# Banded attention scores over all 128 rows with zero-padded keys, a 128-column rotary key projection, and five key slots

## The chip, the cores and the metric

The kernel runs on the 8 cores of one Trainium2 chip. Each core works on four of the 32 sequences and there is no communication. The metric is the device time of the slowest core, in microseconds (us).

Some executions fall into a second, slower state in which one die (cores 0 to 3 or 4 to 7) or both run at a lower granted TensorE clock. Two readings are therefore used. The first is the ratio of fast runs to fast runs. The second is what I call the *undisturbed-die mean*: the mean span of the four cores of a die, over the unprofiled executions in which that die's mean granted clock was 0.990 or more. It also uses the good die of a run whose other die was slow. It is not the metric: the slowest of eight cores lies some 10 to 20 us above it.

## The reference, cut to what matters

A decoder layer: half-step SwiGLU, two attention groups on one input projection (a latent-attention group "MLA" and a sliding-window group "SWA"), an output projection, another half-step SwiGLU. The two feed-forwards are most of the work. The part touched by the change is the scores of the sliding-window group:

```python
SWA_HEADS, SWA_KV_HEADS, SWA_HEAD_DIM, WINDOW = 8, 2, 64, 128

def swa_group(q, k, v, sinks, rel_bias):          # blocks of 128 queries
    q = q.reshape(B, nb, WINDOW, SWA_KV_HEADS, G, dh)      # dh = 64, G = 4
    kb, vb = band(k), band(v)                     # previous block + current block
    s = jnp.einsum('bnqhgd,bnkhd->bnhgqk', q, kb) * (dh ** -0.5)
    ...                                           # bias, mask, softmax with sinks, times vb

# mla_group: k_pe = rope(ckv_pe[..., KV_LORA:], cos, sin)  # 32 columns, shared by all heads
```

The scores contract over only 64 elements. The rotary key needs 32 projection columns, and another 32 for their rotated halves.

## The kernel before

The program is a list of operations put in order by a scheduler at build time; each engine then runs its own list in that order. The feed-forward of one tile (512 tokens) fills the gaps of the attention ("mixer") of another, so attention matmuls stand singly between long runs of feed-forward matmuls.

```python
VS, _ = sb("VS", [128, 8, 192], BF16)             # values, eight slots of 128 tokens
ksT, _ = sb("ksT", [128, 8, 128], BF16)           # keys: group 0 on rows 0-63, group 1 on rows 64-127
...
slot0 = (4 * ti) % 8                              # a tile fills four slots, the next tile the other four
...
proj(w, 192, 128, 64, bka)                        # rotary key projection, 64 columns of the array
k.tt("dve", t1[0:32, :], PS[bka][0:32, :], rope[0:32, 0, :], ALU.mult)
k.tt("dve", t2[0:32, :], PS[bka][32:64, :], rope[32:64, 1, :], ALU.mult)
...
k.copy("act", ksT[:, slot0:slot0 + 4, :].rearrange("p a b -> p (a b)"), PS[bk][:])
...
def swa_scores(q):                                # j: block of 128 queries, g: key-value group
    j, g = units[q]
    for wh in ([0] if 4 * ti + j > 0 else []) + [1]:      # previous block, own block
        kbs = (slot0 + j - 1 + wh) % 8
        _, sb_ = sbk.next()
        k.mm([(PS[sb_][:], ksT[64 * g:64 * g + 64, kbs, :],           # 64 rows of the array
               QS[64 * g:64 * g + 64, :, j * 128:(j + 1) * 128], True, True)])
        k.act(f_[:], PS[sb_][:], AF.Exp, scale=SC_SWA)
        ...
def wload(src, ncol, key):                        # a feed-forward weight tile
    i, w = wr.next()
    k.dma(f"w{i}", w[:, 0:ncol], src, [key], [w[:, 0:ncol]], ncol * 256, dv=-WLEAD)
```

The softmax here doesn't subtract the row's maximum and nothing guards it: scores larger than these inputs give would overflow.

Of the kernel before, what the change touches and what calls it, by code (L numbers as in the profile page):

```python
# [10 lines left out]
BF16 = mybir.dt.bfloat16  # L11
AF = mybir.ActivationFunctionType
ALU = mybir.AluOpType
# [14 lines left out]
WLEAD = 40.0  # L28
# [363 lines left out]
def build_program(NSEQ, debug=False):  # L392
# [26 lines left out]
    with contextlib.ExitStack() as es:  # L419
        es.enter_context(nc.allow_low_precision("bf16 matmul operands, fp32 accumulation"))  # L420
        sc = Sched(nc, es)
        k = K(sc)
        off = [16512]

        def sb(name, shape, dt, at=None):
            n = int(np.prod(shape[1:])) * (2 if dt == BF16 else 4)
            if at is None:
                o = (off[0] + 255) // 256 * 256
                off[0] = o + n
                assert off[0] <= 229344, (name, off[0])  # L430
            else:
                o = at
            t = sc.sb_at(name, shape, dt, o)
            return t, o

        KT, KT_o = sb("KT", [128, 8, S], BF16)
        VA, VA_o = sb("VA", [128, 16, 4, 192], BF16)
        VS, _ = sb("VS", [128, 8, 192], BF16)
        ksT, _ = sb("ksT", [128, 8, 128], BF16)
        EB, EB_o = sb("EB", [128, 2, 8, 128], F32)  # L440
        actb, _ = sb("act", [128, NFC, T], BF16)
        uF, _ = sb("uF", [128, 8, T], BF16)
        uM, uM_o = sb("uM", [128, 8, T], BF16)
        Nb, _ = sb("Nb", [128, 4, T], F32, at=uM_o)
        HB, HB_o = sb("HB", [128, 8, T], F32)
        QT, QT_o = sb("QT", [128, 8, T], BF16)
        uO, _ = sb("uO", [128, 8, T], BF16, at=QT_o)
        QS, QS_o = sb("QS", [128, 4, T], BF16)
        Db, D_o = sb("Db", [128, 4, T], F32)
        cqn, _ = sb("cqn", [128, 2, T], BF16, at=D_o)  # L450
        ckvn, _ = sb("ckvn", [128, T], BF16, at=D_o + 2048)
        kper, _ = sb("kper", [128, T], BF16, at=D_o + 3072)
        rope, _ = sb("rope", [128, 2, T], F32, at=D_o + 4096)
# [14 lines left out]
        sqb, _ = sb("sqb", [128, T], BF16)  # L468
        rsF, _ = sb("rsF", [128, T], F32)
        rsM, _ = sb("rsM", [128, T], F32)  # L470
        rsH, _ = sb("rsH", [128, T], F32)
        cst, _ = sb("cst", [128, 47], F32)
        esink, _ = sb("esink", [128, 4], F32)
        ones, _ = sb("ones", [128, 128], BF16)
        epsb, _ = sb("epsb", [128, 1], F32)
# [16 lines left out]
        PS = [sc.psum(i) for i in range(8)]  # L492
# [35 lines left out]
        a = first * ff  # L528
        for n in range(NT):
            b = min(st_[n + 1] * ff, starts[("F2", n)] - END)  # L530
            if n == 0:
                b = starts[("F2", 0)] - END
# [3 lines left out]
            a = max(b, 4 * ff)  # L536

        def vmap(f):
            v = f
            for a, b, m in windows:  # L540
                v += m * min(max((f - a) / (b - a), 0.0), 1.0)
            return v
# [17 lines left out]
        def load_x(ring, nm, src, key, dv=-8.0):  # L560
            i, t = ring.next()
            k.dma(f"{nm}{i}", t[:], src, [] if key is None else [key], [t[:]], 262144, dv=dv)
            return i, t
# [79 lines left out]

        def wload(src, ncol, key):
            i, w = wr.next()
            k.dma(f"w{i}", w[:, 0:ncol], src, [key], [w[:, 0:ncol]], ncol * 256, dv=-WLEAD)
            return w

        HBl = [HB[:, c, :] for c in range(8)]
# [36 lines left out]
        def ffn_thread():  # L686
# [3 lines left out]
            for ph, n, dur in phases:  # L690
# [36 lines left out]
                elif ph == "P":  # L727
                    for lc in range(NFC):
                        yield vmap(f0 + 2 * fgu * lc / NFC)
                        w = wload(wgu_s[0][lc], 2048, ("wgu", 0, lc))  # L730
                        gate_up(w, uFl, actl, lc, lc == 0)
                        gate_up(w, uF2, act2, lc)
# [3 lines left out]
                    for dc in range(8):  # L736
                        yield vmap(f0 + 2 * fgu + 2 * fdn * dc / 8)
                        ws = [wload(wd_s[0][2 * dc + hf], WD, ("wd", 0, 2 * dc + hf)) for hf in range(2)]
                        for q in range(2):
                            _, bk = fb.next()  # L740
                            for hf in range(2):
                                down_half(ws[hf], (actl, act2)[q], bk, hf)
                            f1_resid(n[q], dc, bk, sts[q])
# [33 lines left out]
        def bg_thread():  # L777
            yield vmap(2 * ff) + 0.5
            k.memset("pool", VA[:].rearrange("p b c e -> p (b c) e")[:, 0:16, 64:128], 1.0)
            k.memset("pool", VS[:, :, 64:128], 1.0)  # L780
            ebf = EB[:].rearrange("p w h q -> p (w h q)")
            k.dma("eb", ebf, relb_in, [], [ebf], 1 << 20)
            k.act(ebf, ebf, AF.Exp)
            k.mask(EB[:, 0], [[0, 8], [-1, 128]], -1, 1, ALU.is_ge)
            k.mask(EB[:, 1], [[0, 8], [1, 128]], 0, -1, ALU.is_ge)
            k.act(esink[:], cst[:, 43:47], AF.Exp)
# [21 lines left out]
        def wkeys(key):  # L808
            return [key, key + (0,), key + (1,)]

        def cload(p):
            i, w = cr.next()
            n = PIECES[p]
            k.dma(f"c{i}", w[:, 0:n], wm_s[p, :, 0:n], wkeys(("wm", p)), [w[:, 0:n]], n * 256, dv=-12.0)
            return w

        def mixer(n):
            si, ti = divmod(n, NTI)
            a, b, m = windows[n]
# [3 lines left out]
            def at(us=0.0):  # L823
                v = vmap(a + (b - a) * min(done[0] / tot, 1.0))
                done[0] += us
                return v
            c0 = ti * T
            slot0 = (4 * ti) % 8
            yield at(0)
            k.dma("rsM", rsM[:], rs_s[n], [("rs", n)], [rsM[:]], 262144, dv=-6.0)  # L830
            for c in range(8):
                _, t = load_x(xmr, "xm", h1_s[n, c], ("h1", n, c))
# [3 lines left out]
            def proj(w, ld, lo, M, bk):  # L836
                w3 = w[:, 0:8 * ld].rearrange("p (k f) -> p k f", k=8)
                for q in (0, 4):
                    k.mm([(PS[bk][0:M, :], w3[:, kc, lo:lo + M], uM[:, kc, :], kc == 0, kc == 7)
                          for kc in range(q, q + 4)])  # L840
            P1 = 1.726
            w = cload(1)
            yield at(P1)
            _, bka = mbk.next()
            proj(w, 192, 128, 64, bka)
            _, t1 = pfr.next()
            _, t2 = pfr.next()
            k.tt("dve", t1[0:32, :], PS[bka][0:32, :], rope[0:32, 0, :], ALU.mult)
            k.tt("dve", t2[0:32, :], PS[bka][32:64, :], rope[32:64, 1, :], ALU.mult)
            k.tt("dve", kper[0:32, :], t1[0:32, :], t2[0:32, :], ALU.add)  # L850
            for hd in range(8):
                k.copy("pool", KT[64:96, hd, c0:c0 + T], kper[0:32, :])
# [1 line left out]
            _, bkv = mbk.next()  # L854
# [4 lines left out]
            w = cload(0)  # L859
            bq = []  # L860
            st = Stats(2, 1.0 / 256, rsH, sqa[1])
            for c in range(2):
                yield at(P1)
                _, bk = mbk.next()
# [5 lines left out]
            w = cload(2)  # L870
            yield at(P1)
            _, bk = mbk.next()
            proj(w, 256, 0, 128, bk)
            k.copy("act", ksT[:, slot0:slot0 + 4, :].rearrange("p a b -> p (a b)"), PS[bk][:])
            w3 = w[:].rearrange("p (k f) -> p k f", k=8)
            _, bk = mbk.next()
            for j in range(4):
                yield at(0.8)
                k.mm([(PS[bk][:, j * 128:(j + 1) * 128], uM[:, kc, j * 128:(j + 1) * 128], w3[:, kc, 128:256],
                       j == 0 and kc == 0, kc == 7) for kc in range(8)])  # L880
            k.copy("act", VS[:, slot0:slot0 + 4, :].rearrange("p b (a d) -> p b a d", a=3)[:, :, 0::2, :],
                   PS[bk][:].rearrange("p (b a d) -> p b a d", b=4, a=2))
            for p in range(2):
                w = cload(3 + p)
                for c in range(2):
                    yield at(P1)
                    _, bk = mbk.next()
                    proj(w, 256, 128 * c, 128, bk)
                    k.copy("act", QS[:, 2 * p + c, :], PS[bk][:])
            w = cload(6)  # L890
            for pr in range(4):
                yield at(0.22)
                _, bk = mbk.next()
# [3 lines left out]
            for j in range(4):  # L897
                yield at(0.22)
                _, bk = mbk.next()
# [5 lines left out]
            w = cload(5)  # L905
# [4 lines left out]
            for qd in range(2):  # L910
                yield at(0.86)
                _, ba = mbk.next()
                _, bb = mbk.next()
                qmm(ba, 512 + qd * 128)
                qmm(bb, 768 + qd * 128)
                _, t1 = pfr.next()
                _, t2 = pfr.next()
                k.tt("dve", t1[:], PS[ba][:], rope[:, 0, :], ALU.mult)
                k.tt("dve", t2[:], PS[bb][:], rope[:, 1, :], ALU.mult)
                _, p_ = ptr_.next()  # L920
# [3 lines left out]
            for pr in range(4):  # L924
                yield at(0.43)
                _, bk = mbk.next()
# [67 lines left out]
            def swa_scores(q):  # L994
                j, g = units[q]
                its[q] = []
                for wh in ([0] if 4 * ti + j > 0 else []) + [1]:
                    kbs = (slot0 + j - 1 + wh) % 8
                    _, sb_ = sbk.next()
                    k.mm([(PS[sb_][:], ksT[64 * g:64 * g + 64, kbs, :],  # L1000
                           QS[64 * g:64 * g + 64, :, j * 128:(j + 1) * 128], True, True)])
                    _, f_ = pfr.next()
                    k.act(f_[:], PS[sb_][:], AF.Exp, scale=SC_SWA)
                    _, p_ = ptr_.next()
                    k.tt("dve", p_[:], f_[:], EB[:, wh, 4 * g:4 * g + 4, :].rearrange("p h q -> p (h q)"), ALU.mult)
                    its[q].append((kbs, p_))
# [18 lines left out]
            for q in range(4):  # L1025
                w = cload(7 + q)
                w3 = w[:].rearrange("p (k f) -> p k f", k=8)
                for c in range(2):
                    yield at(P1)
                    dc = 2 * q + c  # L1030
                    _, bk = mbk.next()
# [3 lines left out]
                    i, t = load_x(xmr, "xm", h1_s[n, dc], ("h1", n, dc))  # L1035
# [8 lines left out]
        def mixer_thread():  # L1044
            for n in range(NT):
                yield from mixer(n)
# [8 lines left out]
        while heap:  # L1055
            v, i = heapq.heappop(heap)
# [117 lines left out]
```

## Time and profile before

| | before |
|---|---|
| median, first 3 runs | 5141.6 us (5140.4 to 5153.8) |
| profiled execution | one die at clock 0.948 |
| core used for reading (core 3, undisturbed die) | 5142.4 us, clock 0.988 |
| PE busy there | 4973.1 us, 97% |

The profiled execution was disturbed on one die. The view of cores of the kernel before, cut:

```profile
core 3: 5142.4 us, clock 0.988
core 6: 5330.1 us, clock 0.948
die 0 (median of its cores): 5123.8 us, clock 0.989
die 1 (median of its cores): 5294.3 us, clock 0.948
```

So I read core 3, whose span is that of an ordinary run. Two parts of its page, busy times and the chain of work that ended last:

```profile
PE 4973.1 (97%) x23180; PEld 2207.4 (43%) x23180; DVE 2336.9 (45%) x3418; ACT 2624.0 (51%) x4303; POOL 1184.2 (23%) x1483
...
## 4 chain that ended last, share of the span: by engine, by line
PE 79%; DMA 10%; DVE 3%; issue 2%; POOL 2%; ACT 2%; SPq 2%; DVEq 0%; POOLq 0%; ACTq 0%
```

PE is busy 97% and is 79% of the chain. The other engines are at half or less. Now to how well PE is used while it is "busy". A matmul's bar in the timeline is longer than its turn, because matmuls overlap, so the *start-to-start* time is what to read. This is the PE timeline of core 3 before (columns: start in us, length of the bar in us, engine, source line, what it writes and reads, rows*columns of the array, the moving operand, count):

```profile
start us, us, engine line op out<-in xcount [idle before <-releaser]
510.20 0.38 PE L324 MATMUL ps<-sb_uF_2_118,sb_W_69 128*128 128x512 bf16 x1
510.42 0.38 PE L324 MATMUL ps<-sb_uF_3_119,sb_W_69 128*128 128x512 bf16 x1
510.73 0.39 PE L324 MATMUL ps<-sb_QS,sb_ksT 64*128 64x512 bf16 x1
511.05 0.39 PE L324 MATMUL ps<-sb_uF_4_120,sb_W_69 128*128 128x512 bf16 x1
511.28 0.38 PE L324 MATMUL ps<-sb_uF_5_121,sb_W_69 128*128 128x512 bf16 x1
```

Full matmuls with 512 columns start 0.21 to 0.22 us apart. The score matmul (`sb_ksT`, 64 rows) starts 0.31 us after its predecessor, and its successor starts 0.32 us after it (the next one 0.23). No idle time is marked: the loss sits inside "busy". The same view around the rotary key projection, which runs in groups of four matmuls on 64 columns of the array:

```profile
start us, us, engine line op out<-in xcount [idle before <-releaser]
1595.69 2.10 PE L324 MATMUL ps<-sb_act,sb_W_69 128*128 128x512 bf16 x9
1597.72 2.02 PE L324 MATMUL ps<-sb_uM,sb_C_70 128*64 128x512 bf16 x8
1599.58 0.59 PE L324 MATMUL ps<-sb_uM,sb_C_71 128*128 128x512 bf16 x2
```

From 1595.69 to 1597.72, the way in, nine full matmuls take 2.03 us where 9 x 0.2155 = 1.94 is usual. The next line merges eight matmuls by name and shows the shape of the first: by their own records in the trace the first four have 64 columns (they are half of the projection) and the other four are full. These eight, with the way out in the middle, take 1.86 us where 1.72 is usual. The matmuls and evictions on the key tile (columns: minimum/median/maximum ns, first and last start, forms):

```profile
engine op xcount: duration ns min/median/max, first and last start us, forms
L324 PE MATMUL ps<-sb_QS,sb_ksT x248: 372/386/387, 506.7 to 4947.3; 64*128 64x512 bf16 x124
L339 ACT CAST sb_ksT<-ps x16: 577/586/587, 367.5 to 4711.3; 128x512 bf16<-128x512 f32 x16
```

A 64-row matmul's own bar (386 ns) is as long as that of a full one.

### The profile page before, as it was taken

How to read it: one execution, taken by the hardware profiler on the slowest of the kernel's cores; microseconds unless marked ns; L12 is line 12 of the kernel's file. 1: busy time of each engine (PE TensorE's matmuls, PEld its weight loads, DVE VectorE, ACT ScalarE, POOL GpSimd, SP SyncE). 2: the span in 40 equal slices, each digit the busy share in tenths (PEclk: the TensorE clock that was granted, in tenths of full speed). 3: DMA queues.
4: the chain of work that ended last, by engine and by line, in shares of the span. 5: the costliest groups of instructions: out<-in, count | busy, mean ns of one | idle time of the engine just before them, and what ended most of it. 6: DMA issues, size and time to landing. Idle time of an engine off the chain costs nothing.

```text
span 5330.1 us, 76556 instructions; the slowest of 8 cores (5113.1 to 5330.1 us)
## 1 busy us (share of the span) xinstructions
PE 5142.6 (96%) x22722; PEld 2257.2 (42%) x23180; DVE 2339.7 (44%) x3418; ACT 2625.8 (49%) x4303; POOL 1182.5 (22%) x1483
## 2 busy tenths in 40 slices
PE   7998899999999999999999999999999999999998
PEld 3443344444444444444444444444444444434433
DVE  3335336354255444353446445353556344243242
ACT  2225354564646363555646373645745553534541
POOL 2334331212112212112122122121132221111110
PEclk9999999999999999999999999999999988888887
DMA  8888967557364757365574747465477545464444
GB/s 268 254 274 259 289 199 217 162 167 234 123 207 165 247 161 234 127 212 177 158 236 152 238 139 253 149 212 171 135 251 232 179 154 161 134 193 132 125 155 135
DMA packets 385167, 1022.11 MB, mean 192 GB/s; under 512 B 42880, under 2 KB 47488, under 8 KB 381312
## 3 DMA queue, kind: packets, MB, share of 16 engines
q1 hardware_dynamic: 384768, 1017.18, 60.6%
q8 instruction: 202, 3.31, 0.3%
q14 instruction: 197, 1.61, 0.1%
HBM read 858.55 MB, written 158.47 MB: 191 GB/s over the span
## 4 chain that ended last, share of the span: by engine, by line
PE 81%; DMA 9%; DVE 2%; issue 2%; POOL 2%; ACT 2%; SPq 1%; DVEq 0%; POOLq 0%; ACTq 0%
PE ps L324 81%; DMA sb_stB_124<-wgu 2%; DMA sb_XM_64<-h1s 1%; SPq L373 1%; DMA sb_XM_65<-h1s 1%; DMA sb_C_70<-wms 1%; ACT L332 1%; POOL sb_KT L343 1%; DVE sb_uM L349 0%; DMA h1s<-sb_XF_63 0%; DMA sb_C_71<-wms 0%; POOL sb_sqb L357 0%; DVE sb_uO L349 0%; POOL sb_obB_126 L343 0%; DMA sb_stB_125<-wd 0%
## 5 line engine op out<-in xcount | busy, mean ns | idle before, releaser
L324 PE MATMUL ps<-sb_uF,sb_W_68 128*128 128x512 bf16 x2581 | 647.1, 393 | 11.9 <-DVE sb_tb_81 L349 5.2
L324 PE MATMUL ps<-sb_uF,sb_W_66 128*128 128x512 bf16 x2586 | 646.7, 392 | 10.1 <-DVE sb_uF L349 3.4
L324 PE MATMUL ps<-sb_uF,sb_W_69 128*128 128x512 bf16 x2585 | 642.2, 391 | 4.9 <-DVE sb_tb_80 L349 1.2
L324 PE MATMUL ps<-sb_uF,sb_W_67 128*128 128x512 bf16 x2577 | 636.7, 391 | 9.3 <-DVE sb_tb_80 L349 4.8
L332 ACT ACT_TABLE_LOAD x357 | 458.0, 1283 | 131.0 <-PE ps L324 112.1
L349 DVE SCALAR_TENSOR_TENSOR sb_tb_80<-sb_tb_80,ps 128x512 f32<-128x512 f32 x352 | 241.6, 686 | 628.8 <-ACT sb_tb_80 L332 627.5
L349 DVE SCALAR_TENSOR_TENSOR sb_tb_81<-sb_tb_81,ps 128x512 f32<-128x512 f32 x352 | 241.6, 686 | 579.5 <-ACT sb_tb_81 L332 576.7
L324 PE MATMUL ps<-sb_QT,sb_KT 96*128 96x512 bf16 (+3 forms) x1280 | 424.2, 357 | 3.7 <-POOL sb_QT L343 1.2
L324 PEld LDWEIGHTS ps<-sb_uF,sb_W_68 128*128 128x128 bf16 x2640 | 259.9, 100 | 335.6 <-issue 107.3
L324 PEld LDWEIGHTS ps<-sb_uF,sb_W_67 128*128 128x128 bf16 x2640 | 260.6, 100 | 331.1 <-issue 93.1
L324 PEld LDWEIGHTS ps<-sb_uF,sb_W_66 128*128 128x128 bf16 x2640 | 260.0, 100 | 331.1 <-issue 101.2
L324 PEld LDWEIGHTS ps<-sb_uF,sb_W_69 128*128 128x128 bf16 x2640 | 259.2, 100 | 327.9 <-issue 95.7
L332 ACT ACTIVATE sb_tb_81<-ps 128x512 f32<-128x512 f32 x352 | 210.0, 597 | 358.2 <-PE ps L324 356.0
L332 ACT ACTIVATE sb_tb_80<-ps 128x512 f32<-128x512 f32 x352 | 209.9, 596 | 327.8 <-PE ps L324 325.6
L324 PE MATMUL ps<-sb_act,sb_W_67 128*128 128x512 bf16 x1294 | 324.1, 397 | 9.3 <-POOL sb_W_67 L343 4.0
L324 PE MATMUL ps<-sb_act,sb_W_66 128*128 128x512 bf16 x1293 | 328.2, 395 | 3.7 <-DMA sb_W_66<-wd2s 1.8
L324 PE MATMUL ps<-sb_act,sb_W_68 128*128 128x512 bf16 x1294 | 325.4, 392 | 5.4 <-DVE sb_XF_63 L349 3.2
L324 PE MATMUL ps<-sb_act,sb_W_69 128*128 128x512 bf16 x1290 | 320.3, 394 | 4.1 <-DMA sb_W_69<-wd1s 2.2
L357 DVE TENSOR_TENSOR sb_act<-sb_tb_80,ps 128x512 bf16<-128x512 f32 x352 | 241.2, 685 | 148.8 <-PE ps L324 141.1
L357 DVE TENSOR_TENSOR sb_act<-sb_tb_81,ps 128x512 bf16<-128x512 f32 x308 | 211.2, 686 | 128.2 <-PE ps L324 121.0
L357 POOL TENSOR_TENSOR sb_sqa_84<-sb_sqa_84,sb_sq_83 128x512 f32<-128x512 f32 x124 | 161.7, 1304 | 431.8 <-ACT sb_sq_83 L332 405.5
L357 POOL TENSOR_TENSOR sb_sqa_85<-sb_sqa_85,sb_sq_82 128x512 f32<-128x512 f32 x81 | 105.5, 1302 | 593.1 <-ACT sb_sq_82 L332 590.8
(452 smaller groups left out, 7294.6 us busy)
## 6 DMA issues: line engine op xcount, KB each, us to landing
sb_W_68<-wgu2s SPq DMA_DIRECT2D x89, 512.0 KB, 3.5
sb_W_69<-wgu2s SPq DMA_DIRECT2D x89, 512.0 KB, 3.5
sb_W_66<-wgu2s SPq DMA_DIRECT2D x87, 512.0 KB, 3.3
sb_W_67<-wgu2s SPq DMA_DIRECT2D x87, 512.0 KB, 3.6
sb_W_66<-wgu1s SPq DMA_DIRECT2D x72, 512.0 KB, 4.5
sb_W_67<-wgu1s SPq DMA_DIRECT2D x72, 512.0 KB, 4.3
sb_C_71<-wms SPq DMA_DIRECT2D x72, 512.0 KB, 5.6
sb_C_70<-wms SPq DMA_DIRECT2D x72, 512.0 KB, 5.6
```

The lines of the kernel that those rows point to most:

```text
L324: inst = nc.tensor.matmul(out, lhsT=lt, rhs=r, start=st, stop=sp, skip_group_check=True)
L332: return self.sc.op("act", lambda: nc.scalar.activation(out=out, in_=in_, func=func, scale=scale, **kw), 0.2 + nfree(out) / 1200, rd, [out ...
L343: return self.sc.op("pool", lambda: nc.gpsimd.tensor_copy(out=out, in_=in_), 0.2 + n * 1.03 / 1200, [in_], [out], dv=dv)
L349: return self.sc.op("dve", lambda: nc.vector.scalar_tensor_tensor(out=out, in0=in0, scalar=scalar, in1=in1, op0=op0, op1=op1), (nfree(out) ...
L357: return self.sc.op(eng, lambda: e.tensor_tensor(out=out, in0=in0, in1=in1, op=op), (n + 151) / 960 if eng == "dve" else 0.25 + n * 2.6 / ...
L373: return self.sc.op("sp", lambda: nc.sync.dma_start(out=out, in_=in_), 0.07, reads, writes, dma=sem, nbytes=nbytes, dv=dv, tmin=tmin)
```

## The change

The intent is to make every 64-row and 64-column matmul of the kernel a full-array one (the 96-row ones stay). Keys get a layer for each group with zeros in the other group's 64 rows, so that the score matmul can contract over 128 rows, queries of both groups included. The rotary key projection takes the 64 columns before it along (their result is not used) and its own 64 then land on rows 64 to 127. The padded keys would need twice the memory, so there are five slots rather than eight, and the last block of a tile is carried into slot 0. The weight load also gains dependences on the two halves of the converted weights.

```diff
--- before.py
+++ after.py
@@ -435,8 +435,8 @@
 
         KT, KT_o = sb("KT", [128, 8, S], BF16)
         VA, VA_o = sb("VA", [128, 16, 4, 192], BF16)
-        VS, _ = sb("VS", [128, 8, 192], BF16)
-        ksT, _ = sb("ksT", [128, 8, 128], BF16)
+        VS, _ = sb("VS", [128, 5, 192], BF16)
+        ksT, _ = sb("ksT", [128, 2, 5, 128], BF16)
         EB, EB_o = sb("EB", [128, 2, 8, 128], F32)
         actb, _ = sb("act", [128, NFC, T], BF16)
         uF, _ = sb("uF", [128, 8, T], BF16)
@@ -643,7 +643,7 @@
 
         def wload(src, ncol, key):
             i, w = wr.next()
-            k.dma(f"w{i}", w[:, 0:ncol], src, [key], [w[:, 0:ncol]], ncol * 256, dv=-WLEAD)
+            k.dma(f"w{i}", w[:, 0:ncol], src, wkeys(key), [w[:, 0:ncol]], ncol * 256, dv=-WLEAD)
             return w
 
         HBl = [HB[:, c, :] for c in range(8)]
@@ -778,6 +778,8 @@
             yield vmap(2 * ff) + 0.5
             k.memset("pool", VA[:].rearrange("p b c e -> p (b c) e")[:, 0:16, 64:128], 1.0)
             k.memset("pool", VS[:, :, 64:128], 1.0)
+            k.memset("pool", ksT[64:128, 0], 0.0)
+            k.memset("pool", ksT[0:64, 1], 0.0)
             ebf = EB[:].rearrange("p w h q -> p (w h q)")
             k.dma("eb", ebf, relb_in, [], [ebf], 1 << 20)
             k.act(ebf, ebf, AF.Exp)
@@ -825,7 +827,6 @@
                 done[0] += us
                 return v
             c0 = ti * T
-            slot0 = (4 * ti) % 8
             yield at(0)
             k.dma("rsM", rsM[:], rs_s[n], [("rs", n)], [rsM[:]], 262144, dv=-6.0)
             for c in range(8):
@@ -842,11 +843,11 @@
             w = cload(1)
             yield at(P1)
             _, bka = mbk.next()
-            proj(w, 192, 128, 64, bka)
+            proj(w, 192, 64, 128, bka)
             _, t1 = pfr.next()
             _, t2 = pfr.next()
-            k.tt("dve", t1[0:32, :], PS[bka][0:32, :], rope[0:32, 0, :], ALU.mult)
-            k.tt("dve", t2[0:32, :], PS[bka][32:64, :], rope[32:64, 1, :], ALU.mult)
+            k.tt("dve", t1[0:32, :], PS[bka][64:96, :], rope[64:96, 0, :], ALU.mult)
+            k.tt("dve", t2[0:32, :], PS[bka][96:128, :], rope[96:128, 1, :], ALU.mult)
             k.tt("dve", kper[0:32, :], t1[0:32, :], t2[0:32, :], ALU.add)
             for hd in range(8):
                 k.copy("pool", KT[64:96, hd, c0:c0 + T], kper[0:32, :])
@@ -871,14 +872,18 @@
             yield at(P1)
             _, bk = mbk.next()
             proj(w, 256, 0, 128, bk)
-            k.copy("act", ksT[:, slot0:slot0 + 4, :].rearrange("p a b -> p (a b)"), PS[bk][:])
+            if ti:
+                k.copy("pool", ksT[:, :, 0, :], ksT[:, :, 4, :])
+                k.copy("pool", VS[:, 0, :], VS[:, 4, :])
+            k.copy("act", ksT[0:64, 0, 1:5, :].rearrange("p a b -> p (a b)"), PS[bk][0:64, :])
+            k.copy("dve", ksT[64:128, 1, 1:5, :].rearrange("p a b -> p (a b)"), PS[bk][64:128, :])
             w3 = w[:].rearrange("p (k f) -> p k f", k=8)
             _, bk = mbk.next()
             for j in range(4):
                 yield at(0.8)
                 k.mm([(PS[bk][:, j * 128:(j + 1) * 128], uM[:, kc, j * 128:(j + 1) * 128], w3[:, kc, 128:256],
                        j == 0 and kc == 0, kc == 7) for kc in range(8)])
-            k.copy("act", VS[:, slot0:slot0 + 4, :].rearrange("p b (a d) -> p b a d", a=3)[:, :, 0::2, :],
+            k.copy("act", VS[:, 1:5, :].rearrange("p b (a d) -> p b a d", a=3)[:, :, 0::2, :],
                    PS[bk][:].rearrange("p (b a d) -> p b a d", b=4, a=2))
             for p in range(2):
                 w = cload(3 + p)
@@ -995,10 +1000,9 @@
                 j, g = units[q]
                 its[q] = []
                 for wh in ([0] if 4 * ti + j > 0 else []) + [1]:
-                    kbs = (slot0 + j - 1 + wh) % 8
+                    kbs = j + wh
                     _, sb_ = sbk.next()
-                    k.mm([(PS[sb_][:], ksT[64 * g:64 * g + 64, kbs, :],
-                           QS[64 * g:64 * g + 64, :, j * 128:(j + 1) * 128], True, True)])
+                    k.mm([(PS[sb_][:], ksT[:, g, kbs, :], QS[:, :, j * 128:(j + 1) * 128], True, True)])
                     _, f_ = pfr.next()
                     k.act(f_[:], PS[sb_][:], AF.Exp, scale=SC_SWA)
                     _, p_ = ptr_.next()
```

## The prediction

> **What bounds it now.** PE. The profiled execution fell in the slow state (the view of cores: die 0 at clock 0.989, median 5124 us; die 1 at 0.948, 5294 us), so I read core 3: 5142.4 us, like the 5141.6 us median. There PE is busy 97% (4973 us), ACT 51%, DVE 45%, POOL 23%; 79% of the chain that ended last is PE matmul. PE time is nearly the whole time.
>
> **What the change takes away.** In the PE timeline of core 3 successive 512-column matmuls start 0.2155 us apart (the Trainium skill, "TensorE: Matmul & The Clock Gate", Back-to-back issue gap, gives N/2.4 + 2.5 ns; the trace agrees). I subtracted that amount from every start-to-start time:
> - full to 64-row (banded scores): +95 ns, 214 times; back to full: +101 ns, 215 times. Example: 64-row start 510.73 us, next start 511.05.
> - full to 64-column (rotary key projection): +93 ns (23 of 32; the others hide behind real waits); back: +95 ns, 32 times.
> - 64-row to 64-row of the same row group: +10 ns, 28 times; five pairs of different row groups started together, saving 213 ns each.
> - 96-row matmuls: within 5 ns, no penalty.
>
> The skill's "TensorEngine Tiling (Array Packing)", Key Properties, says changing the tiling mode drains the engine; this trace shows about 95 ns in and 100 out. Full-size matmuls of as many columns stream just as long, so the extra rows and columns cost nothing.
>
> Removed: 215x0.101 + 214x0.095 = 42.0; 64-column 23x0.093 + 32x0.095 = 5.2; same-group pairs 0.3; lost pairing 5x0.213 = -1.1. About **46 us of PE, 0.9%**.
>
> **What it adds.** Per tile (16): one 64x512 DVE eviction (about 0.7 us, as other 512-column DVE work here) beside the ACT one, which keeps its 585 ns; in 12 tiles two small POOL carries (estimated below 0.6 us each, from the 607 ns of the 32x512 POOL copies); two POOL memsets early, while POOL idles 3.5 us for the first weights. Both engines have room. Five slots end the double buffering of the keys, but a tile's key projection follows the previous tile's output projection, so the slots are free by then; only the eviction now waits for the carries. The added dependences on converted weights are free: the last conversion write of the second gate/up weights is issued at 553 us, their first load at 611. Instruction order changes only locally: 361 lines of 6470 on PE, most just the shape.
>
> **Critical path.** I take 90% of 46 us to come through, the rest being spent in waits for ACT, POOL masks and DMA that PE reaches sooner: 42 us.
>
> **Prediction: 5100 us**, 8 in 10 between 5080 and 5125. Faster by over 2%: 0.02; within 2%: 0.96; slower by over 2%: 0.02.
>
> **What would show it.** On a fast core: spacing around the key-score matmuls and the rotary projection 0.215 us, not 0.31 to 0.32; other PE idle unchanged (about 170 us); clock near 0.99; no PE wait over 1 us behind the new POOL copies and DVE evictions. The column part alone would save about 5 us, the row part about 41.
>
> **What would make it wrong.** If the excess is not the mode change but a wait for the score bank or an ACT result, it stays. If the local reordering, or the carry queued behind long POOL adds (1.3 us), delays the key eviction and holds a PSUM bank, PE waits eat the gain. A lower granted clock with the filled array would too: 1% of clock is 50 us.

## More of the kernel before

The waits of PE before, the two largest (columns: total us, times, longest us):

```profile
engine line waited for: us in total, times, longest us
PE ps L324 <- POOL sb_sqb L357: 26.1, 21, 5.3
PE ps L324 <- DVE sb_uM L349: 24.3, 14, 4.8
```

## The result, and the profile after

| | before | after |
|---|---|---|
| median | 5141.0 us (4 runs) | 5108.5 us (4 runs, one of them slow: 5928.9) |
| ratio of fast runs | 1 | 0.9928, 95% interval 0.9906 to 0.9950 |
| undisturbed-die mean, ± standard error | 5118.7 ± 0.8 us (28 dies) | 5083.2 ± 1.2 us (7 dies) |
| PE busy, core read | 4973.1 us | 4922.4 us |
| PE not busy, core read | 169 us | 189 us |

A ratio is the mean time of one kernel's fast runs over the mean of the other's fast runs of the same rounds, so it is not quite the ratio of the medians in the first row. The median after counts the slow run; the median of the three fast runs alone is 5104.7 us, 36.3 below before. The undisturbed-die means pool all executions of a kernel, so they mix chips; they say 35.5 us.

The profiled execution of the changed kernel was a fast one. The view of cores after, cut:

```profile
core 0: 5070.9 us, clock 0.993
core 5: 5111.3 us, clock 0.989
die 0 (median of its cores): 5085.5 us, clock 0.992
die 1 (median of its cores): 5094.8 us, clock 0.991
```

The cores of one execution differ by 40 us among themselves, as much as the change is worth. That is why the text below never compares two single cores' spans. The page of the slowest core after, the same two parts:

```profile
PE 4922.4 (96%) x23180; PEld 2225.9 (44%) x23180; DVE 2347.5 (46%) x3434; ACT 2626.3 (51%) x4303; POOL 1195.3 (23%) x1509
...
## 4 chain that ended last, share of the span: by engine, by line
PE 76%; DMA 12%; DVE 4%; issue 2%; ACT 2%; POOL 2%; SPq 1%; DVEq 0%; POOLq 0%; ACTq 0%
```

PE busy time fell by 50.7 us, from 4973.1 to 4922.4, in spite of 248 score matmuls and 128 rotary ones that use more of the array. (Two different cores: by their clock records core 3 before spent 62 us at 0.81 of the clock and core 5 after 24 us, so some 7 us of the 50.7 are clock; the table below is free of that.) The timeline after, at the same place in the order of instructions:

```profile
507.79 0.38 PE L324 MATMUL ps<-sb_uF_2_118,sb_W_69 128*128 128x512 bf16 x1
508.01 0.38 PE L324 MATMUL ps<-sb_uF_3_119,sb_W_69 128*128 128x512 bf16 x1
508.23 0.38 PE L324 MATMUL ps<-sb_QS,sb_ksT 128*128 128x512 bf16 x1
508.44 0.38 PE L324 MATMUL ps<-sb_uF_4_120,sb_W_69 128*128 128x512 bf16 x1
```

The score matmul now starts 0.22 us after its predecessor and its successor 0.21 after it. The rotary projection after:

```profile
1584.96 2.53 PE L324 MATMUL ps<-sb_act,sb_W_69 128*128 128x512 bf16 x11 [2.27 <-DMA sb_W_69<-wd1s]
1587.33 1.89 PE L324 MATMUL ps<-sb_uM,sb_C_70 128*128 128x512 bf16 x8
1589.06 1.89 PE L324 MATMUL ps<-sb_uM,sb_C_71 128*128 128x512 bf16 x8
```

Eleven full matmuls take 2.37 us and the eight that begin with the four of the projection 1.73 us, which is 0.2155 each. The key tile after:

```profile
L324 PE MATMUL ps<-sb_QS,sb_ksT x248: 376/379/380, 502.9 to 4917.3; 128*128 128x512 bf16 x124
L339 ACT CAST sb_ksT<-ps x16: 566/579/580, 363.4 to 4683.2; 64x512 bf16<-64x512 f32 x16
L341 DVE CAST sb_ksT<-ps x16: 694/694/696, 363.7 to 4683.2; 64x512 bf16<-64x512 f32 x16
L343 POOL COPY sb_ksT<-sb_ksT x12: 396/397/679, 366.5 to 4549.9; 128x256 bf16<-128x256 bf16 x12
...
who waited for it (us, times):
  POOL sb_ksT L343: 17.0, 8
```

The new eviction on DVE takes 694 ns, each carry about 397 ns, the ACT eviction is hardly shorter for half the rows (579 against 586 ns at the median), and the two memsets end before POOL has other work. In the second part, "who waited", POOL's carry waits 17.0 us in all for PE to finish with the old slots, but in the view of PE's waits of this core nothing waits for the key tile. The waits of PE after:

```profile
PE ps L324 <- DVE sb_uM L349: 29.6, 13, 7.7
PE ps L324 <- POOL sb_sqb L357: 26.8, 24, 5.2
```

These grew a little or stayed. To put numbers on both effects I took all start-to-start times of PE, subtracted columns/2.4 + 2.4 ns for each matmul, and split the rest: at changes of shape (to or from a 64-row or 64-column matmul, at most 105 ns each), and waits (rests of over 150 ns). Only cores with all 23180 matmuls recorded are used. The row "before's order" is a profile of the kernel before with nothing but its extra dependences changed (experiment `keys_only`), since the profile of before was disturbed.

| us per core | changes of shape | waits over 150 ns |
|---|---|---|
| before, core 3 (494 changes) | 48.7 | 202 |
| before's order, mean of 6 cores | 48.8 | 194.5 |
| after, mean of 6 cores | 0.0 | 204.6 |

The changes of shape are gone entirely. On the means some 10 us of the 48.8 reappear as longer waits, but the cores of one profile spread widely (176 to 211 in before's order, 191 to 226 after), so the 10 is uncertain by about 8. Three experiments below lean the same way: 196.7 us in before's order (`col_only`), 208.1 and 201.9 in the changed order (`after_again`, `eight_keys`); `shape64` does not, as told at its second profile. The count leaves out a small tail: the second matmul after a change, of whatever shape, starts about 10 ns late (the median over 214 full ones, and over 28 on 64 rows; before, core 3), some 2 us in all; and before had five pairs of 64-row matmuls that ran at once, which saved 1.1 us and are lost.

### The profile page after: what moved, and what is told of

It reads as the page before. It is cut to its first block, busy times and chain, and to the rows that moved or that the text cites. A ratio compares the mean times of both kernels' runs of the same rounds, so it can differ in the third digit from the quotient of the medians.

```text
span 5111.3 us, 77134 instructions; the slowest of 8 cores (5070.9 to 5111.3 us)
## 1 busy us (share of the span) xinstructions
PE 4922.4 (96%) x23180; PEld 2225.9 (44%) x23180; DVE 2347.5 (46%) x3434; ACT 2626.3 (51%) x4303; POOL 1195.3 (23%) x1509
## 4 chain that ended last, share of the span: by engine, by line
PE 76%; DMA 12%; DVE 4%; issue 2%; ACT 2%; POOL 2%; SPq 1%; DVEq 0%; POOLq 0%; ACTq 0%
PE ps L324 76%; DMA sb_stB_124<-wgu 2%; DMA sb_XM_64<-h1s 2%; DMA sb_XM_65<-h1s 1%; SPq L373 1%; DMA sb_C_71<-wms 1%; DMA sb_C_70<-wms 1%; ACT L332 1%; DMA sb_stB_125<-wm 1%; DVE sb_uO L349 1%; DMA sb_stB_125<-wd 1%; DVE sb_HB L349 1%; POOL sb_sqb L357 1%; DVE sb_uM L349 0%; DMA sb_W_66<-wgu1s 0%
## 5 line engine op out<-in xcount | busy, mean ns | idle before, releaser
L324 PE MATMUL ps<-sb_uF,sb_W_66 128*128 128x512 bf16 x2640 | 627.4, 381 | 6.1 <-DVE sb_uF L349 3.5
L324 PE MATMUL ps<-sb_uF,sb_W_68 128*128 128x512 bf16 x2640 | 626.0, 380 | 6.4 <-DVE sb_tb_81 L349 3.7
L324 PE MATMUL ps<-sb_uF,sb_W_69 128*128 128x512 bf16 x2640 | 623.9, 380 | 1.8 <-DVE sb_tb_80 L349 1.8
L324 PE MATMUL ps<-sb_uF,sb_W_67 128*128 128x512 bf16 x2640 | 619.1, 379 | 6.6 <-DVE sb_tb_80 L349 5.7
L324 PE MATMUL ps<-sb_QT,sb_KT 96*128 96x512 bf16 (+3 forms) x1280 | 413.4, 348 | 0.5 <-ACT sb_PT_74 L332 0.5
L324 PEld LDWEIGHTS ps<-sb_uF,sb_W_66 128*128 128x128 bf16 x2640 | 256.7, 98 | 313.0 <-issue 18.5
L324 PEld LDWEIGHTS ps<-sb_uF,sb_W_67 128*128 128x128 bf16 x2640 | 256.4, 98 | 313.2 <-issue 12.8
L324 PEld LDWEIGHTS ps<-sb_uF,sb_W_68 128*128 128x128 bf16 x2640 | 255.8, 98 | 313.8 <-issue 18.1
L324 PEld LDWEIGHTS ps<-sb_uF,sb_W_69 128*128 128x128 bf16 x2640 | 257.0, 98 | 309.1 <-issue 11.5
L324 PE MATMUL ps<-sb_act,sb_W_68 128*128 128x512 bf16 x1320 | 316.0, 381 | 5.9 <-DVE sb_XF_63 L349 3.2
L324 PE MATMUL ps<-sb_act,sb_W_67 128*128 128x512 bf16 x1320 | 310.5, 382 | 11.4 <-POOL sb_W_67 L343 7.3
L324 PE MATMUL ps<-sb_act,sb_W_66 128*128 128x512 bf16 x1320 | 314.0, 379 | 2.2 <-POOL sb_W_66 L343 2.2
L324 PE MATMUL ps<-sb_act,sb_W_69 128*128 128x512 bf16 x1320 | 308.4, 380 | 3.2 <-DMA sb_W_69<-wd1s 2.3
L357 POOL TENSOR_TENSOR sb_sqa_84<-sb_sqa_84,sb_sq_83 128x512 f32<-128x512 f32 x124 | 162.1, 1307 | 390.5 <-ACT sb_sq_83 L332 363.5
L341 DVE COPY sb_Nb<-ps 64x512 f32<-64x512 f32 x256 | 175.6, 686 | 123.3 <-PE ps L324 118.8
```

Source lines behind the costliest of these rows:

```text
L324: inst = nc.tensor.matmul(out, lhsT=lt, rhs=r, start=st, stop=sp, skip_group_check=True)
L341: return self.sc.op("dve", lambda: nc.vector.tensor_copy(out=out, in_=in_), (n + 151) / 960, [in_], [out], dv=dv)
L357: return self.sc.op(eng, lambda: e.tensor_tensor(out=out, in0=in0, in1=in1, op=op), (n + 151) / 960 if eng == "dve" else 0.25 + n * 2.6 / ...
```

## The experiments

Theory A: a matmul on 64 rows or 64 columns between full ones costs PE about 95 ns going in and 100 ns coming out, and not paying this is the gain; what did not arrive went into waits that PE reaches sooner. Rivals: B, the gain came from the new order of instructions or the evictions; C, the column part carries much of it; D, the carry and the five slots ate part of it; E, the added dependences matter.

Undisturbed-die means in one place (mean ± standard error, number of dies):

| kernel | mean, us | dies | changes of shape in its trace, us |
|---|---|---|---|
| before | 5118.7 ± 0.8 | 28 | 48.7 |
| keys_only | 5116.7 ± 2.1 | 3 | 48.8 |
| col_only | 5117.8 ± 1.1 | 9 | 42.5 |
| shape64 | 5116.4 ± 1.8 | 8 | 42.5 |
| row_only | 5085.2 ± 0.9 | 7 | 6.3 |
| after | 5083.2 ± 1.2 | 7 | 0 |
| eight_keys | 5082.8 ± 1.4 | 8 | 0 |
| pair64 | 5108.8 ± 1.1 | 6 | 24.7, less the pairs' overlap |
| dose | 5202.2 ± 2.5 | 7 | 140.1 |

These means pool chips, and the chips differ: before stands at 5120.6 ± 0.8 us on chip 7 (14 dies), 5116.2 ± 1.3 on chip 5 (12) and 5119.7 on chip 2 (2). So a difference of a few us between kernels that ran on different chips is not shown by the table. On chip 7 alone: before 5120.6, `col_only` 5117.8 ± 1.1 (9 dies), `shape64` 5118.1 ± 2.0 (6), `row_only` 5085.2 ± 0.9 (7), after 5080.1 ± 2.2 (only 2). On chip 5 alone: before 5116.2, `keys_only` 5116.7 ± 2.1, `eight_keys` 5082.8 ± 1.4, `pair64` 5108.8 ± 1.1, `dose` 5203.0 ± 0.6 (5). The chip of the changed kernel's first runs (5 of its 7 dies) is not on record.

### shape64: only the 64-row matmuls put back

```diff
-k.mm([(PS[sb_][:], ksT[:, g, kbs, :], QS[:, :, j * 128:(j + 1) * 128], True, True)])
+k.mm([(PS[sb_][:], ksT[64 * g:64 * g + 64, g, kbs, :],
+       QS[64 * g:64 * g + 64, :, j * 128:(j + 1) * 128], True, True)])
```

> The changed kernel with one thing put back: each banded score matmul reads only its own 64 rows of the padded keys and of the queries. Order of the instructions on every engine is identical to the changed kernel's, and the results are right. Theory A (the 64-row matmuls cost PE about 100 ns going in and 100 coming out, and that was the gain): the excess of 95 to 103 ns comes back 420 to 430 times, 41 us of PE, and the time rises by 30 to 41 us over the changed kernel, to about 0.998 to 1.000 of the kernel before. Rival B (the gain came from the new order of instructions, the split eviction or the slots): the time stays within 5 us of the changed kernel.

Measured: correct; ratio of fast runs to before 1.0015 (0.9951 to 1.0080), three fast runs: 5133.7, 5135.3, and 5179.1 in which one die's clock was 0.983. Undisturbed dies 5116.4 us, 33.2 above the changed kernel. The timeline of core 3 of this run:

```profile
502.65 1.03 PE L324 MATMUL ps<-sb_uF,sb_W 128*128 128x512 bf16 x4
503.61 0.39 PE L324 MATMUL ps<-sb_QS,sb_ksT 64*128 64x512 bf16 x1
503.93 0.82 PE L324 MATMUL ps<-sb_uF,sb_W 128*128 128x512 bf16 x3
```

The four full matmuls before the score matmul take 0.96 us instead of 0.86, and 0.32 us pass after it: the excess is back, 42.5 us at 430 changes. Evictions, carries, slots, order of instructions and bank use are those of the changed kernel. So the shape alone makes about nine tenths of the gain (33.2 ± 2.2 of 35.5 us), and B falls. It also says how much a microsecond of this excess is worth: 33.2 of 42.5, or 0.78; on chip 7 alone 38.0 ± 2.9, or 0.89.

### col_only and row_only: one part at a time

```diff
 # col_only, on the kernel before; row_only is the changed kernel with this reversed
-proj(w, 192, 128, 64, bka)
+proj(w, 192, 64, 128, bka)
-k.tt("dve", t1[0:32, :], PS[bka][0:32, :], rope[0:32, 0, :], ALU.mult)
-k.tt("dve", t2[0:32, :], PS[bka][32:64, :], rope[32:64, 1, :], ALU.mult)
+k.tt("dve", t1[0:32, :], PS[bka][64:96, :], rope[64:96, 0, :], ALU.mult)
+k.tt("dve", t2[0:32, :], PS[bka][96:128, :], rope[96:128, 1, :], ALU.mult)
```

> The kernel before with only the rotary key projection made 128 columns wide; order on all engines as before. Theory A: 23 clean entries of 93 ns and 32 exits of 95 ns go, 5 us, so a ratio of 0.999 to the kernel before, at most 0.9985. Rival B: 1.000. The difference is near the noise; the start-to-start times of the trace decide whether the excess is gone.

> The changed kernel with the rotary key projection put back to 64 columns; order as in the changed kernel. Theory A: the 64-column excess comes back, 5 us at most, so a ratio of 0.993 to 0.995 to the kernel before, against 0.993 for the changed kernel. Rival C (the column part carries a good part of the gain, for example through a larger wait): 0.996 or more.

Measured: both correct; col_only 0.9999 (0.9977 to 1.0021), row_only 0.9924 (0.9900 to 0.9948). By undisturbed dies the column part gains 0.9 ± 1.4 us alone and 2.0 ± 1.5 us on top of the row part, while its excess of 6.3 us is gone from the trace. C falls: the row part is nearly all of the gain, 33.5 us. Whether the column part brought less than the 5 us I had counted is not shown: by the pooled means it did, but on chip 7 alone, where `col_only` and `row_only` ran, it gains 2.9 ± 1.3 us alone and 5.2 ± 2.4 on top of the row part. Half of its 32 entries in before (16, on core 3) start over 0.3 us later than the usual spacing, up to 5 us, at the start of a tile's attention where PE waits anyway. What is saved there can be spent in the next such wait; if little came through, this may be why, but that is a reading of the trace, not a test.

### after_again: the yardstick

> The changed kernel itself, on the same chip as its relatives, as their yardstick. All theories: ratio 0.991 to 0.995 to the kernel before. In the trace no excess beside the score matmuls and the rotary projection.

Measured: correct, but five of its six executions were slow, so there is no ratio. The one fast run, which was the profiled one, took 5123.0 us. The two good dies of the slow, unprofiled runs are pooled into the changed kernel's mean above, and the profile shows no change of shape and waits of 208.1 us, near the 204.6 of the first profile.

### eight_keys: no carry of keys

```diff
-ksT, _ = sb("ksT", [128, 2, 5, 128], BF16)
+ksT, _ = sb("ksT", [128, 2, 8, 128], BF16)
-    k.copy("pool", ksT[:, :, 0, :], ksT[:, :, 4, :])
+# slot0 = (4 * ti) % 8 again; evictions to slot0..slot0+3; reads (slot0 + kbs - 1) % 8
+# two small constants moved into another tile's padding, to make room
```

> The changed kernel with eight key slots again, padded, and no carry of keys (the carry of values stays). It tells where the part of the 46 us went that did not arrive. Theory A (absorbed in waits that were there before): same as the changed kernel within 5 us, undisturbed dies near 5082 us. Rival D (the POOL carry and the eviction that waits for it hold PE up): 6 to 10 us faster, undisturbed dies at 5072 to 5076 us.

Measured: correct; 0.9933 (0.9910 to 0.9955); undisturbed dies 5082.8 us, 0.4 below the changed kernel, though on other chips; on its own chip it is 33.5 ± 2.0 below before. The 6 to 10 us that D asked for are not there, so D falls for the keys. The carry of values stayed, as memory had no room for eight slots of both; it was not tested alone. But `shape64`, which has everything of the change but the row shape, is 1.4 ± 2.1 us *faster* than `col_only`, which has none of it but the column shape (on chip 7 alone 0.3 ± 2.2 slower). So all the additions together cost nothing that can be seen.

### keys_only: the added dependences

```diff
-k.dma(f"w{i}", w[:, 0:ncol], src, [key], [w[:, 0:ncol]], ncol * 256, dv=-WLEAD)
+k.dma(f"w{i}", w[:, 0:ncol], src, wkeys(key), [w[:, 0:ncol]], ncol * 256, dv=-WLEAD)
```

> The kernel before with only the added dependences of the weight loads on the converted weights; order on all engines as before. Theory A: ratio 1.000 within 0.001, since the conversions are written long before. Rival E (these waits cost or save something): a difference of over 0.002 and new waits of PE for the weight tiles.

Measured: correct; ratio 1.0035, interval 0.9985 to 1.0084, so the ratio misses the 0.001 I asked for and does not decide by itself: of three fast runs one took 5165.1 us with one die at clock 0.989. The undisturbed dies (three only) stand at 5116.7, against 5116.2 for before on the same chip. No effect of E is seen, with an uncertainty of 2.4 us.

### dose and dose_again: the same excess, elsewhere and larger

One matmul in each gate/up group of the feed-forwards reads 64 of its rows. The result is wrong (relative error 0.106); count, columns and order stay.

```diff
-k.mm([(PS[bk][:], w4[:, aa, kc, :], u[kc], kc == 0, kc == 7)
+k.mm([(PS[bk][:], w4[:, aa, kc, :], u[kc], kc == 0, kc == 7) if (aa, kc) != (1, 5) else
+      (PS[bk][:], w4[0:64, aa, kc, :], u[kc][0:64], False, False)
       for kc in range(lo, lo + step)])
```

> Wrong result on purpose. The changed kernel with one matmul in each gate/up group of the feed-forwards (352 in all, the sixth of the second eight) reading 64 of its 128 rows; count, columns and the order of instructions on every engine are unchanged. Theory A: each costs 95 ns in and 101 ns out wherever it stands, so 69 us more of PE in the start-to-start times. If PE time comes through whole, +69 us over the changed kernel; if four fifths come through, as the 34 us of the undisturbed dies against 42.5 us of excess say for the run with the 64-row scores put back, +55 us. Rival B (the excess belongs to the score matmuls, their banks and their ACT readers, not to the change of shape): no excess, time within 5 us of the changed kernel.

The count in this expectation was wrong by a factor of two: both feed-forwards pass through that code, so there are 704 such matmuls and 139 us of excess are to be expected. The run itself stands. Its profile fell in the slow state, so it was taken again:

> Wrong result on purpose. The kernel with 64-row matmuls in the gate/up groups once more, for a profile in the fast state. My first count was wrong: there are 704 such matmuls, not 352, as both feed-forwards go through this code. Expected: 1408 changes of shape at 96 and 103 ns, 139 us; the undisturbed dies of the first run stood at 5203 us, 119 to 121 us over the changed kernel, so waits of PE some 20 us shorter than the changed kernel's, 185 us or so.

Measured: one fast run of each, 5217.2 and 5222.6 us; undisturbed dies 5202.2 us, 119 above the changed kernel. The fast profile, the group of these matmuls by form on core 1, with no idle time in front of them (last number):

```profile
L324 PE MATMUL ps<-sb_uF,sb_W 64*128 64x512 bf16 x704 | 272.4, 387 | 0.0
```

Its timeline, twelve feed-forward matmuls in a row of which one is of this kind:

```profile
1401.47 2.96 PE L324 MATMUL ps<-sb_uF,sb_W 128*128 128x512 bf16 x12
1404.27 0.38 PE L324 MATMUL ps<-sb_QT,sb_KT 96*128 96x512 bf16 x1
```

They take 2.80 us instead of 12 x 0.2155 = 2.59. Over the trace the median excess is 96 ns in and 103 ns out, the same figures as at the score matmuls, though these share neither banks nor readers with them. So the excess belongs to the change of shape and not to the attention. 119 of 140.1 us came through, or 0.85 (against `eight_keys` on the same chip, 120 us or 0.86). The waits over 150 ns fell to 178 us (mean of the six complete cores) from 204.6: PE arrives later everywhere and waits less. This is the absorption of theory A run backwards.

### pair64: two 64-row matmuls at once

The other way to make use of 64 rows is to give both halves of the array something to do.

```diff
-k.mm([(PS[sb_][:], ksT[:, g, kbs, :], QS[:, :, j * 128:(j + 1) * 128], True, True)])
+k.mm([(PS[sbs[g]][:], ksT[64 * g:64 * g + 64, g, kbs, :],
+       QS[64 * g:64 * g + 64, :, j * 128:(j + 1) * 128], True, True) for g in range(2)], both=True)
+# both groups of a block in one operation, two banks; products with V one block later
```

> Right result; the other way to use 64 rows: the two key-value groups' score matmuls of a block issued back to back into two banks, so that they run at the same time on the two halves of the rows. From the trace of before (five such pairs started 2 ns apart): per pair 95 + 2 + 216 + 101 = 414 ns against 2 x 216 = 432 ns padded, so 2 us less of PE in all, nothing that can be told apart. The order of instructions changes widely, so plus or minus 15 us from other waits: ratio to before 0.990 to 0.996. If the pairs do not run at the same time, 27 us more: ratio 0.996 to 1.000.

Measured: correct; too few fast runs for a ratio (5126.6 and 5145.2 us); undisturbed dies 5108.8 us, 25.6 above the changed kernel. The timeline of core 1:

```profile
506.63 0.81 PE L326 MATMUL ps<-sb_act,sb_W 128*128 128x512 bf16 x3
507.37 0.39 PE L326 MATMUL ps<-sb_QS,sb_ksT 64*128 64x512 bf16 x2
507.69 3.63 PE L326 MATMUL ps<-sb_act,sb_W 128*128 128x512 bf16 x16
```

The two matmuls of a pair start together (one bar of 0.39 us for two; 0.32 us to the next start): 3 or 4 ns apart in 121 of core 1's 124 pairs, at most 6. (The expectation says 2 ns; the five pairs of before started 3 to 4 ns apart too.) PE's account is as expected: 12.1 us in, 13.1 out (24.7 together in the table, where each change counts at most 105 ns), 26.3 saved by overlap, so 1 us better than padded. The time is not: against before on the same chip the undisturbed dies give 0.9986, outside the 0.990 to 0.996 that was expected for pairs that run at once. The waits over 150 ns are 235.9 us against 204.6. Two things changed that could make them: the order of instructions is another one, and each pair takes both of the two score banks at once. They were not tested apart. One wait of core 1 does not stand among the changed kernel's:

```profile
PE ps L326 <- DMA sb_uF<-u2s: 11.4, 1, 11.4
```

This run says two things: pairing costs PE what padding costs, and what comes with it here, new order and bank use together, costs 26 us, most of what the change gains. Whether pairing could be scheduled without these waits is open.

### before_again and shape64_again: profiles that did not settle it

> The kernel before once more, for a profile in the fast state (the first one was slow). Expected: 48 to 49 us of excess at 494 changes of shape, and 190 to 200 us of longer waits of PE on the cores whose traces are complete, about 10 less than the changed kernel's two traces (205 and 208).

> The changed kernel with the 64-row score matmuls put back, once more, since its first profile was of a run 14 us longer than its siblings. If the part of the gain that did not arrive was absorbed in waits that PE now reaches sooner, the excess of 42.5 us stands beside waits of 195 to 200 us, less than the changed kernel's 205 to 208. If the new order or the carry made the waits, they are 205 us or more here too, and the undisturbed dies stand near 5127 us, not 5117.

Measured: the single execution of before fell in the slow state on both dies (clock 0.82, 5966.9 us), so it gives no waits to compare. The split at 105 ns does not hold at that clock either (its 51.7 us is the cap, 494 times); over the usual spacing there, 263 ns, the median excess is 107 ns in and 103 out for 64 rows (core 3). The second profile of shape64 had one good die, at 5130.9 us, again longer than the good dies of the unprofiled executions of the same job (5110.2 and 5112.3 us). Its waits are 207.6 us (three complete cores; 214.3 on the good die of the first profile), which is what the rival expected, while the unprofiled spans near 5116 us are what absorption expected. The profiled runs of shape64 are both about 14 us longer than its other runs, so its wait sums speak for longer runs; I trust the spans, but the traces of shape64 do not confirm the absorption. The dose run does, so the account of the missing part stays in part open.

No version that beats the changed kernel came out of this: `eight_keys` equals it and `pair64` is slower.

## Why the prediction was right

The predicted time was 5100 us, 5080 to 5125, within 2%; measured 5108.5 us (5104.7 over the fast runs alone), ratio 0.9928.

- *What bounds it*: right. PE time moved the kernel's time, at 0.78 (`shape64`) and 0.85 (`dose`) of its size.
- *The excess is the change of shape*: right, shown by `shape64` (only the shape differs) and by `dose` (same 96 and 103 ns in the feed-forward).
- *Its size, 46 us of PE*: right in the trace; 48.7 us by the fuller count, which leaves out the 1.1 us of the lost pairs, all gone after.
- *The additions are free*: right, shown for the carry of keys (`eight_keys`) and for all of them together (`shape64` against `col_only`). The carry of values was not tested alone. PE shows no wait on the key tile after.
- *The row part about 41 us, the column part about 5 us*: the row part gave 33 us (35 to 38 on chip 7 alone), the column part 1 to 2 (2.9 ± 1.3 and 5.2 ± 2.4 on chip 7 alone). I had counted 23 of the 32 column entries as clean, and a recount gives 16; that takes only 0.7 us off the 5.2. Whether the column term was mis-sized beyond that stays open.
- *90% comes through, 42 us*: probably too high, and it was a guess, not worked out. For the row shape the runs say 0.78 to 0.89 (`shape64`) and 0.85 (`dose`); the whole change brought 32.5 us by the medians (36.3 with fast runs alone), 35.5 by the undisturbed dies, 37 by the ratio, and 40.6 ± 2.3 on chip 7 alone, where the changed kernel has two dies. That the time came close is helped by 46 us being a little too low where 90% was a little too high. I wrote that "other PE idle" would stay near 170 us; the core read after has 189.
- *Clock near 0.99*: right, in the fast state, before and after.

Where each microsecond of the missing part waits is not shown. `dose` shows its sum, the table of waits points the same way within its spread, and the profiles of `shape64` contradict it; the waits are the same few (for the first normalised activations, for the POOL sums, for weights) that were there before.

## What to carry to other kernels

When PE looks fully busy, read the start-to-start times around matmuls of an odd shape: here the cost of changing between full and 64-row or 64-column shapes did not show as idle time, and a lone 64-row matmul of 512 columns took as long as a full one plus about 200 ns. Padding the small operand with zeros removed it at no PE cost where such matmuls stood singly; count the changes of shape, not the matmuls, to know what is at stake. Then expect less than all of it (here between 0.7 and 0.9, by which kernels and chips are compared) where PE has other waits left to run into, and be careful with a rewrite that shuffles the order of instructions: `pair64`, which did, came out 26 us slower than padding. And compare kernels on one chip: here chips differed by 4 us, as much as the whole column part.

## What the Trainium skill lacked or had wrong

- "TensorEngine Tiling (Array Packing)", Key Properties, says that a change of tiling mode drains the engine and gives no figure. The runs: 95 to 96 ns in and 101 to 103 ns out for 64 rows, 93 to 95 ns each way for 64 columns. It does not say that 96 rows count as full: the 1280 such matmuls stood at a median of 0 to 4 ns over the usual spacing. Nor that the second matmul after a change, full or 64-row, still starts about 10 ns late.
- "TensorE: Matmul & The Clock Gate", Back-to-back issue gap, gives about 131 ns per matmul as the sustained pace of weight-load and matmul pairs at 512 columns, and calls columns/2.4 + 2.5 ns the isolated gap. Here pairs sustained 215 to 216 ns over thousands of matmuls; the "isolated" formula is the one that fits.
- The same page, Part 1, Seeing it yourself, expects 13/16 of the clock (0.8125) once three cores of a die run dense matmuls, for as long as the load lasts. Here all eight did, and the cores of undisturbed dies ran at a mean of about 0.99. The level agrees, its permanence does not: the means below that are mixtures. Core 5 of the first profile of before (mean 0.947) stood at 0.81 for its first 1000 us and at 0.97 to 1.00 in every stretch of 500 us after; core 3 of `before_again` (mean 0.823) stayed at 0.81 from 500 us to the end; core 0 of the changed kernel (0.993) was never below 0.97 in a stretch of 500 us. No page says that this state comes and goes between executions of the same kernel.
